# One place in memory for every moved operand: two kinds of activation slots in a single-core decoder step

## The chip, the core and the metric

The kernel runs on one core of one Trainium2 chip. The metric is device time in microseconds for one execution; three runs of the kernel before have a median of 1624.26 us (1624.0 to 1624.49). The profile is of one execution.

## The reference

One step of a one-layer decoder for 256 prompt tokens and 8 x 4 sample tokens, 288 tokens in all, with a model width of 2048. All arrays are float32. Cut to what matters:

```python
mod = (silu(c) @ w_ada + b_ada)          # 6 shifts, scales and gates of 2048, per group of tokens
h = rms(x, g_mix) * (1 + sc_m) + sh_m
proj = h @ w_in                          # 2048 x 9216: b, c, hc, u, v, ga, gb
z = c_gate * hc;  ya = b_gate * conv(z)  # short convolution, width 3
yb = gelu(u) * (causal_mix(rms(gelu(v))) + b_sg)
merged = sigmoid(ga) * (ya @ w_pa) + sigmoid(gb) * (yb @ w_pb)
x = x + gt_m * (merged @ w_out)
h2 = rms(x, g_ffn) * (1 + sc_f) + sh_f
gate, up = split(h2 @ w_ffn_in)          # 2048 x 11264
x = x + gt_f * ((silu(gate) * up) @ w_ffn_out)   # 5632 x 2048
```

The outputs are the normed x of both groups, the last rows of z, and the normed v.

## The kernel before

Everything is held with features on the 128 partitions and the 288 tokens along the free axis. A matrix product is cut into tiles of 128 x 128 weights; for each, the weights are loaded into TensorE (the stationary operand) and 288 columns of activations are streamed past them (the moved operand) into one of a few PSUM tiles (`pm`, `px`), which sums over the tiles of the inner dimension.

Float32 precision comes from three products for each tile, written in `triple` (L227 to L236). Both operands are split into a high part, rounded to the type fp32r, and the rest, a low part: the weights into `hi` and `lo` (`Blk.split`, ScalarE's cast at L453, VectorE's subtraction at L459 or L248), the activations into a pair that `split` makes (L299 to L304), or `modulate`, `make_h1` and `scaled_tile`. The three products are high by high (L229), high weights by low activations (L232), and low weights by high activations (L234). In the profile, `pm<-s,hi` at L229 and L232 names the moved operand `s` and the weights `hi`. There are 11,328 matmuls of this kind. Some of them are 298 columns wide: ten columns behind the tokens carry the shift of the modulation through the product.

The activations live in `slots`: 92 buffers that `slot` hands out, each 298 x 4 = 1,192 bytes per partition, whatever is stored in it. Some slots are moved operands (fp32r pairs). Others hold plain float32 results that TensorE does not read in this way: `sinkA` (L733 to L742) copies the first partial product of a column tile m of w_in out of PSUM into a slot, where it stays (`part[m]`) until a later step adds the rest (`sinkC`, `sinkB`, `sinkD`). For m < 48 the slot also keeps the ten extra columns, which `sinkC` and `rescale` use. Small tiles for a short time come from another pool, `tmp`, of five buffers.

In the built program the 92 slots stand 1,216 bytes apart, so that they start at four places modulo 256 bytes: the 11,328 moved operands stand at 32 (2,652 of them), 96 (2,524), 160 (3,196) and 224 (2,956). The weights `hi` and `lo` stand at 224 modulo 256, all of them.

The order of the matmuls on TensorE is the order in which the code writes them. The order on VectorE, ScalarE and SyncE is written by hand in the first part (until the step `free`), and set by a scheduler after it. Weights come from HBM over SyncE's queue into seven `raw` buffers; a buffer comes free when both casts have read it.

Of the kernel before, what the change touches and what calls it, by code (L numbers as in the profile page):

```python
# [8 lines left out]
F32 = mybir.dt.float32  # L9
F32R = mybir.dt.float32r  # L10
BF16 = mybir.dt.bfloat16
ALU = mybir.AluOpType
AF = mybir.ActivationFunctionType

P = 128
D = 2048
T = 288
TP = 256
TU = T + 10
NB = 8  # L20
NS = 4
NC = 9
DFF = 5632
SLOTS = 92
RAW = 7
LEAD = 12
LAG = 2
# [27 lines left out]
SINGLE = 10  # L55
FIRST = 16
ROOTLESS = 48
LATER = 48
ON_VECTOR = (2, 5, 7, 9, 10, 12, 14, 18, 19, 22, 23, 26, 27, 30, 32, 35, 37, 41, 43, 45, 47)
XCUT = (0, 1, 2, 6, 10, 14, 16)  # L60
# [24 lines left out]
def decoder_kernel(tc, d):  # L85
    nc = tc.nc
    from contextlib import ExitStack

    with ExitStack() as es:
        def pool(name, bufs=1, **kw):  # L90
            return es.enter_context(tc.tile_pool(name=name, bufs=bufs, **kw))

        pc = pool("const")
        pw = pool("wstream")
        pslot = pool("slots", SLOTS)
        ptmp = pool("tmp", 5)
        pps = pool("psum", 4, space=bass.MemoryType.PSUM)
        with tc.manual_schedule(engines={nc.tensor.engine}):
            _body(tc, nc, d, pc, pw, pslot, ptmp, pps)


def _body(tc, nc, d, pc, pw, pslot, ptmp, pps):
    ids = [0]

    def nm(s):
        ids[0] += 1
        return f"{s}_{ids[0]}"

    def const(name, shape, dt=F32):
        return pc.tile(shape, dt, tag=name, name=name)  # L110

    def slot(dt=F32, shape=(P, T)):
        return pslot.tile(list(shape), dt, tag="s", name=nm("s"), padded_shape=[P, TU])

    def tmp(n=T):
        return ptmp.tile([P, n], F32, tag="t", name=nm("t"), padded_shape=[P, TU])
# [7 lines left out]
    V, A, G, PE, SY = nc.vector, nc.scalar, nc.gpsimd, nc.tensor, nc.sync  # L124


    ct = const("ct", [P, 16, NC])
    A.dma_start(ct, d["c"])
    cp1 = const("cp1", [P, C1_END])
    A.dma_start(cp1, d["cpack1"])  # L130
# [19 lines left out]
    V.memset(mhalf, -0.5)  # L150
    cs = const("cs", [P, 16, 32])
    V.memset(cs, 0.0)
    ctt = const("ctt", [P, 16, NC])
    A.activation(ctt, ct, AF.Tanh, scale=0.5)
    V.scalar_tensor_tensor(ctt, ctt, 1.0, ct, ALU.add, ALU.mult)
    cs_made = V.tensor_scalar(cs[:, :, :NC], ctt, 0.5, None, ALU.mult)
# [128 lines left out]
    def behind(a, b):  # L285
        tc.add_manual_dep(
            a.ins,
            b.ins.name,
            mybir.DependencyInfo(mybir.DependencyClass.NoSync, mybir.DependencyReason.DATA),
            reason="program order",  # L290
        )

    def sam(ap):
        return ap.rearrange("p (b s) -> p b s", s=NS)

    def bc4(ap):
        return ap.unsqueeze(2).to_broadcast([P, NB, NS])

    def split(a, n=T):  # L299
        hi = slot(F32R, (P, n))  # L300
        A.copy(hi, a)  # L301
        lo = slot(F32R, (P, n))
        V.tensor_tensor(lo, a, hi.bitcast(F32), ALU.subtract)  # L303
        return hi, lo  # L304

    def normed(kt, rb):
        t = slot()
        V.tensor_tensor(t, x[:, kt, :], rb, ALU.mult)
        return t
# [419 lines left out]
        return Do(f)  # L729

    part, raws = {}, {}

    def sinkA(m, ps):  # L733
        t = slot(shape=(P, TU) if m < ROOTLESS else (P, T))
        part[m] = t[:, :T]
        w = T
        if m < ROOTLESS:
            raws[m], w = t, TU
        if m not in ON_VECTOR if m < ROOTLESS else m % 2 or m % 8 == 4:
            A.copy(t[:, :w], ps[:, :w])  # L740
        else:
            V.tensor_copy(t[:, :w], ps[:, :w])  # L742

    def sinkC(m, ps):
        if m not in raws:
            return sinkB(m, ps)
        t = raws.pop(m)
        V.scalar_tensor_tensor(t[:, :TP], ps[:, :TP], t[:, T : T + 1], t[:, :TP], ALU.add, ALU.add)  # L748
        rescale(m + 4, V.tensor_tensor(t[:, TP:T], ps[:, TP:T], t[:, TP:T], ALU.add))

    def rescale(m, after):
        if m in raws:
            t = raws[m]
            behind(V.tensor_tensor(t[:, :T], t[:, :T], S["rb1"], ALU.mult), after)  # L754
            V.tensor_tensor(sam(t[:, TP:T]), sam(t[:, TP:T]), bc4(t[:, T + 1 : T + NC]), ALU.add)

    def sinkX(m, ps):
        after = sinkB(m, ps)
        if m >= 68:
            rescale(m - 68, after)  # L760

    def sinkB(m, ps):
        return V.tensor_tensor(part[m], ps[:, :T], part[m], ALU.add)  # L763
# [318 lines left out]
    a0[1].defer = a1[1].defer = True  # L1082
    a0[1].half = lambda: warm(6)
    w0 = OneTile("w0", 0, xe.__getitem__, sinkA)
    wK = OneTile("wK", 0, xe.__getitem__, lambda j, ps: sinkA(SINGLE + j, ps))
    w0.hooks = {8: [a1[0].run], 11: [a1[1].run, second_tile]}
    many = (ROOTLESS - FIRST) // 8
    wA = [Blk("wA", i, (xe if i < many else h1).__getitem__, lambda m, ps: sinkA(FIRST + m, ps)) for i in range((72 - FIRST) // 8)]
    wB = [Blk("wB", i, rh1, lambda m, ps: sinkB(LATER + m, ps)) for i in range((72 - LATER) // 4)]
    wX = [Blk("wX", i, rh1, lambda m, ps: sinkX(LATER + m, ps)) for i in range((72 - LATER) // 4)]  # L1090
    wS = [Blk("wS", i, rh1, sinkC) for i in range(SINGLE // 2)]
    wC = [Blk("wC", i, rh1, lambda m, ps: sinkC(SINGLE + m, ps)) for i in range((LATER - SINGLE) // 2)]
    for b in wA[:many]:
        b.width = TU
# [56 lines left out]
    n = len(steps)  # L1151
# [167 lines left out]
```

## Time and profile before

| | |
|---|---|
| median of three runs | 1624.26 us |
| the profiled execution | 1624.22 us |
| its span, from first to last instruction | 1622.4 us |
| granted TensorE clock | 0.998 |
| TensorE busy | 1611.5 us (99%), 12,641 matmuls |
| VectorE busy | 1017.0 us (63%) |
| ScalarE busy | 737.3 us (45%) |
| HBM read | 352.74 MB, 219 GB/s over the span |

A busy time is the sum over which an engine had an instruction running. Matmuls overlap: one takes about 295 ns in the trace, but the next one starts long before it ends, so the time that a matmul costs is the distance from its start to the next start. "Chain" is the work that ended last, followed back from the end. A wait is told as who waited for whom.

### The profile page before, as it was taken

To read this page: it belongs to the slowest core of one execution; us is meant where nothing else is said; L and a number is where in the kernel's file an instruction comes from. 1 tells how busy PE (TensorE), PEld (TensorE's weight loads), DVE (VectorE), ACT (ScalarE), POOL (GpSimd) and SP (SyncE) were. 2 spreads that over 40 slices of the span, in tenths; PEclk is the share of its full clock that TensorE was granted. 3 is DMA by queue.
4 is the path that set the end of the run, shared out by engine and by line. 5 is a ranking of instruction groups with operands and counts; after the bars stand their busy time and mean duration, and the time that the engine had idled before them with its cause. 6 is when DMAs were issued, how large, how long until landed. Compare 5 with 4: busy or idle time off the path is not lost.

```text
span 1622.4 us, 31579 instructions
## 1 busy us (share of the span) xinstructions
PE 1611.5 (99%) x12641; PEld 1547.6 (95%) x12641; DVE 1017.0 (63%) x2194; ACT 737.3 (45%) x1360; POOL 21.2 (1%) x65
## 2 busy tenths in 40 slices
PE   9999999999999999999999999999999999999997
PEld 8998999899999999999999999999999999999997
DVE  6676788877755667667744555555555555555565
ACT  5533344643444434456643444444444444444454
POOL 0000000000000000011000000000000000000000
PEclk9999999999999999999999999999999999999999
DMA  9887866777778676654576556443564534645341
GB/s 376 324 319 287 312 237 212 273 279 295 288 281 337 260 271 227 236 176 157 193 304 251 217 177 208 159 172 110 169 224 156 173 117 161 226 157 172 109 162 59
DMA packets 59476, 357.88 MB, mean 221 GB/s; under 512 B 6720, under 2 KB 10176, under 8 KB 28608
## 3 DMA queue, kind: packets, MB, share of 16 engines
q1 hardware_dynamic: 59040, 355.73, 59.8%
q8 instruction: 99, 1.62, 0.4%
q14 instruction: 49, 0.40, 0.1%
q10 hardware_dynamic: 288, 0.13, 0.0%
HBM read 352.74 MB, written 3.09 MB: 219 GB/s over the span
## 4 chain that ended last, share of the span: by engine, by line
PE 98%; DMA 1%; DVE 0%; ACT 0%; DVEq 0%; issue 0%; ACTq 0%
PE pm L229 31%; PE pm L234 30%; PE pm L232 30%; PE ada L393 5%; DMA raw<-in_wK 1%; DMA raw<-in_w 0%; DVE st L1048 0%; DMA ct<-in_c 0%; PE px L232 0%; PE px L229 0%; PE px L234 0%; PE px L880 0%; PE px L879 0%; PE px L826 0%; PE px L203 0%; ACT hi L453 0%
## 5 line engine op out<-in xcount | busy, mean ns | idle before, releaser
L229 PE MATMUL pm<-s,hi 128*128 128x288 f32 (+1 forms) x3750 | 1109.1, 296 | 0.0
L232 PE MATMUL pm<-s,hi 128*128 128x288 f32 (+1 forms) x3750 | 1103.8, 294 | 0.0
L234 PE MATMUL pm<-s,lo 128*128 128x288 f32 (+1 forms) x3738 | 1102.2, 295 | 0.0
L453 ACT CAST hi<-raw 128x512 fp32r<-128x512 f32 (+1 forms) x963 | 587.2, 612 | 803.3 <-PE pm L232 762.6
L459 DVE TENSOR_TENSOR lo<-raw,hi 128x512 fp32r<-128x512 f32 (+1 forms) x849 | 578.7, 683 | 437.9 <-ACT hi L453 425.3
L229 PEld LDWEIGHTS pm<-s,hi 128*128 128x128 f32 x3750 | 705.7, 188 | 15.2 <-issue 13.0
L232 PEld LDWEIGHTS pm<-s,hi 128*128 128x128 f32 x3750 | 704.7, 188 | 0.0
L234 PEld LDWEIGHTS pm<-s,lo 128*128 128x128 f32 x3738 | 702.9, 188 | 0.0
L248 DVE TENSOR_TENSOR lo<-raw,hi 128x512 fp32r<-128x512 f32 x111 | 74.6, 675 | 29.6 <-ACT hi L453 28.9
L393 PE MATMUL ada<-raw,cs 128*32 128x512 f32 (+2 forms) x1152 | 88.3, 452 | 0.2 <-DMA raw<-in_a 0.2
L393 PEld LDWEIGHTS ada<-raw,cs 128*32 128x32 f32 x1152 | 30.9, 110 | 45.0 <-issue 41.1
L771 DVE TENSOR_TENSOR s<-pm,s 128x288 f32<-128x288 f32 x72 | 32.8, 456 | 19.9 <-PE pm L234 19.7
L301 ACT CAST s<-t 128x288 fp32r<-128x288 f32 (+1 forms) x76 | 32.9, 433 | 18.8 <-DVE t L803 12.4
L303 DVE TENSOR_TENSOR s<-t,s 128x288 fp32r<-128x288 f32 (+1 forms) x76 | 34.9, 459 | 6.5 <-ACT s L301 6.4
L343 DVE SCALAR_TENSOR_TENSOR x<-pm,mod,x 128x256 f32<-128x256 f32 x79 | 37.6, 475 | 0.0
L969 DVE SCALAR_TENSOR_TENSOR t<-t,pm 128x288 f32<-128x288 f32 x42 | 19.1, 454 | 20.9 <-PE pm L234 20.9
L763 DVE TENSOR_TENSOR s<-pm,s 128x288 f32<-128x288 f32 x48 | 21.8, 454 | 10.4 <-PE pm L234 9.5
L342 DVE TENSOR_TENSOR t<-pm,mod 128x32 f32<-128x32 f32 x79 | 15.2, 192 | 18.3 <-PE pm L234 18.2
L748 DVE SCALAR_TENSOR_TENSOR s<-pm,s 128x256 f32<-128x256 f32 x48 | 23.1, 480 | 4.1 <-PE pm L234 4.1
L754 DVE TENSOR_TENSOR s<-s,rb 128x288 f32<-128x288 f32 x48 | 21.5, 448 | 0.0
L171 ACT ACTIVATE t<-x 128x288 f32<-128x288 f32 x29 | 12.9, 445 | 17.4 <-DVE x L346 17.4
L176 DVE TENSOR_TENSOR acc<-acc,t 128x288 f32<-128x288 f32 x33 | 15.0, 455 | 8.2 <-ACT t L171 8.2
(164 smaller groups left out, 470.9 us busy)
## 6 DMA issues: line engine op xcount, KB each, us to landing
raw<-in_fi SPq DMA_DIRECT2D x84, 1024.0 KB, 4.8
raw<-in_a SPq DMA_DIRECT2D x64, 1024.0 KB, 7.9
raw<-in_f SPq DMA_DIRECT2D x64, 704.0 KB, 4.0
raw<-in_wD SPq DMA_DIRECT2D x34, 1024.0 KB, 5.4
raw<-in_aE SPq DMA_DIRECT2D x16, 1024.0 KB, 9.6
raw<-in_wo SPq DMA_DIRECT2D x16, 1024.0 KB, 6.0
raw<-in_wC SPq DMA_DIRECT2D x19, 768.0 KB, 4.3
raw<-in_pa SPq DMA_DIRECT2D x8, 1024.0 KB, 5.9
```

The source lines that it names most:

```text
L229: PE.matmul(out, wh, ah, start=first, stop=False)
L232: end_ = PE.matmul(out, wh, al, start=False, stop=turn and last)
L234: end_ = PE.matmul(out, wl, ah, start=False, stop=last)
L248: lows.pop(0)[1]()
L301: A.copy(hi, a)
L303: V.tensor_tensor(lo, a, hi.bitcast(F32), ALU.subtract)
L343: V.scalar_tensor_tensor(x[:, m, :TP], ps[:, :TP], mod[:, gt0 + m, 0:1], x[:, m, :TP], ALU.mult, ALU.add)
L393: PE.matmul(acc[32 * j : 32 * j + 32, :w], cs[:, kt, :], self.raw[:, o : o + w], start=kt == 0, stop=kt == 15, tile_position=(0, 32 * j), ...
L453: A.copy(hi, self.raw[:, s * 128 : e * 128])
L459: sub()
L748: V.scalar_tensor_tensor(t[:, :TP], ps[:, :TP], t[:, T : T + 1], t[:, :TP], ALU.add, ALU.add)
L771: V.tensor_tensor(a, ps[:, :T], a, ALU.add)
```

## The change

The slots are divided in two kinds. `slots` are now 56 buffers with a pitch of 320 elements (1,280 bytes, five times 256), and a slot that will hold an fp32r operand begins 7 elements (28 bytes) behind the buffer's start. `kept` is a new pool of 36 buffers of 288 elements (1,152 bytes) for the long-lived partial products of 36 column tiles, `LONG`: m = 24 to 27 and 40 to 71. Since a `kept` buffer has no room for the ten extra columns, the 12 of these tiles with m < 48 put them into a new constant, `extra`, with a copy of their own, and `raws[m]` holds the pair of both. The tiles `ct` and `ctt`, which were constants, come from the `tmp` pool.

In the built program all 11,328 moved operands then start at 92 modulo 256, and all their weights at 64 modulo 256.

```diff
-SLOTS = 92
+MAIN = 56
+KEPT = 36
+LEADIN = 7
+PITCH = 320
...
+LONG = tuple(range(24, 28)) + tuple(range(40, 72))
...
-        pslot = pool("slots", SLOTS)
+        pslot = pool("slots", MAIN)
+        pkept = pool("kept", KEPT)
...
     def slot(dt=F32, shape=(P, T)):
-        return pslot.tile(list(shape), dt, tag="s", name=nm("s"), padded_shape=[P, TU])
+        o = LEADIN if dt == F32R else 0
+        t = pslot.tile([P, o + shape[1]], dt, tag="s", name=nm("s"), padded_shape=[P, PITCH])
+        return t[:, o:] if o else t
+
+    def kept():
+        return pkept.tile([P, T], F32, tag="k", name=nm("s"))
...
-    ct = const("ct", [P, 16, NC])
+    ct = tmp(16 * NC).rearrange("p (k n) -> p k n", n=NC)
...
-    ctt = const("ctt", [P, 16, NC])
+    ctt = tmp(16 * NC).rearrange("p (k n) -> p k n", n=NC)
...
+    extra = const("extra", [P, sum(m < ROOTLESS for m in LONG), TU - T])
 
     def sinkA(m, ps):
-        t = slot(shape=(P, TU) if m < ROOTLESS else (P, T))
+        wide = m < ROOTLESS and m not in LONG
+        t = kept() if m in LONG else slot(shape=(P, TU) if wide else (P, T))
         part[m] = t[:, :T]
-        w = T
+        w = TU if wide else T
+        copy = A.copy if (m not in ON_VECTOR if m < ROOTLESS else m % 2 or m % 8 == 4) else V.tensor_copy
+        copy(t[:, :w], ps[:, :w])
         if m < ROOTLESS:
-            raws[m], w = t, TU
-        if m not in ON_VECTOR if m < ROOTLESS else m % 2 or m % 8 == 4:
-            A.copy(t[:, :w], ps[:, :w])
-        else:
-            V.tensor_copy(t[:, :w], ps[:, :w])
+            e = t[:, T:] if wide else extra[:, LONG.index(m)]
+            raws[m] = t, e
+            if not wide:
+                copy(e, ps[:, T:TU])
 
     def sinkC(m, ps):
         if m not in raws:
             return sinkB(m, ps)
-        t = raws.pop(m)
-        V.scalar_tensor_tensor(t[:, :TP], ps[:, :TP], t[:, T : T + 1], t[:, :TP], ALU.add, ALU.add)
+        t, e = raws.pop(m)
+        V.scalar_tensor_tensor(t[:, :TP], ps[:, :TP], e[:, :1], t[:, :TP], ALU.add, ALU.add)
...
     def rescale(m, after):
         if m in raws:
-            t = raws[m]
+            t, e = raws[m]
             behind(V.tensor_tensor(t[:, :T], t[:, :T], S["rb1"], ALU.mult), after)
-            V.tensor_tensor(sam(t[:, TP:T]), sam(t[:, TP:T]), bc4(t[:, T + 1 : T + NC]), ALU.add)
+            V.tensor_tensor(sam(t[:, TP:T]), sam(t[:, TP:T]), bc4(e[:, 1:NC]), ALU.add)
```

TensorE's, GpSimd's and SyncE's instructions stand in the same order as before, row for row. VectorE and ScalarE have six more instructions each, the copies into `extra`. On VectorE, where the column tiles m = 26 and 27 are copied out of PSUM (`pm` a PSUM tile, `s` a slot, `q` a sum of squares), there stood before:

```order
L248 TENSOR_TENSOR lo_614<-raw_134,hi_612 128x512
L742 COPY s_627<-pm_618 128x298
L742 COPY s_639<-pm_629 128x298
L592 TENSOR_TENSOR q_122<-q_122,q_123 128x1152
L248 TENSOR_TENSOR lo_638<-raw_134,hi_636 128x512
```

and now, with the changed file's line numbers:

```order
L258 TENSOR_TENSOR lo_619<-raw_138,hi_617 128x512
L750 COPY s_633<-pm_624 128x288
L755 COPY extra<-pm_624 128x10
L750 COPY s_646<-pm_636 128x288
L755 COPY extra<-pm_636 128x10
L602 TENSOR_TENSOR q_126<-q_126,q_127 128x1152
L258 TENSOR_TENSOR lo_645<-raw_138,hi_643 128x512
```

Each copy of 298 columns became one of 288 and one of 10, both ahead of the next instruction in VectorE's order. On ScalarE it is the same at m = 24 and 25. Before:

```order
L453 CAST hi_584<-raw_129 128x512
L740 COPY s_600<-pm_592 128x298
L453 CAST hi_609<-raw_129 128x512
L453 CAST hi_612<-raw_134 128x512
L740 COPY s_615<-pm_602 128x298
```

and now:

```order
L463 CAST hi_588<-raw_133 128x512
L750 COPY s_604<-pm_596 128x288
L755 COPY extra<-pm_596 128x10
L463 CAST hi_614<-raw_133 128x512
L463 CAST hi_617<-raw_138 128x512
L750 COPY s_620<-pm_607 128x288
L755 COPY extra<-pm_607 128x10
```

The casts of the next weights stand behind one short copy more.

More of the change, by code (lines that the diff above doesn't have):

```diff
@@ L98, in decoder_kernel, with _body @@
         with tc.manual_schedule(engines={nc.tensor.engine}):
-            _body(tc, nc, d, pc, pw, pslot, ptmp, pps)
-def _body(tc, nc, d, pc, pw, pslot, ptmp, pps):
+            _body(tc, nc, d, pc, pw, pslot, pkept, ptmp, pps)
+def _body(tc, nc, d, pc, pw, pslot, pkept, ptmp, pps):
     ids = [0]
```

## The prediction

> **What bounds the kernel now.** I read the page first, for the span, the engines and the chain that ended last, then the waits of TensorE.
>
> ```profile
> span 1622.4 us, 31579 instructions
> PE 1611.5 (99%) x12641; PEld 1547.6 (95%) x12641; DVE 1017.0 (63%) x2194; ACT 737.3 (45%) x1360; POOL 21.2 (1%) x65
> PE 98%; DMA 1%; DVE 0%; ACT 0%; DVEq 0%; issue 0%; ACTq 0%
> PE pm L576 <- POOL wb L570: 1.1, 1, 1.1
> PE px L203 <- DVE t L185: 0.6, 1, 0.6
> PE px L232 <- DVE s L692: 0.3, 1, 0.3
> PE ada L393 <- DMA raw<-in_a: 0.2, 1, 0.2
> PE pm L506 <- ACT s L682: 0.2, 1, 0.2
> ```
>
> 98% of the chain is TensorE, and all its waits together are 2.4 us. The time is therefore the number of matmuls times the distance of their starts. By form, the matmuls that the change touches are these (columns: line, engine, operation, output and operands, shape and count; busy us, mean ns):
>
> ```profile
> L229 PE MATMUL pm<-s,hi 128*128 128x288 f32 x3626 | 1071.5, 295 | 0.0
> L234 PE MATMUL pm<-s,lo 128*128 128x288 f32 x3626 | 1068.6, 295 | 0.0
> L232 PE MATMUL pm<-s,hi 128*128 128x288 f32 x3626 | 1066.5, 294 | 0.0
> L229 PE MATMUL pm<-s,hi 128*128 128x298 f32 x124 | 37.6, 303 | 0.0
> L232 PE MATMUL pm<-s,hi 128*128 128x298 f32 x124 | 37.2, 300 | 0.0
> L234 PE MATMUL pm<-s,lo 128*128 128x298 f32 x112 | 33.5, 299 | 0.0
> ```
>
> With the small groups they are 11,328. Now the groups in the window from 1200 to 1300 us, where nothing but them runs on TensorE:
>
> ```profile
> L234 PE MATMUL pm<-s,lo 128*128 128x288 f32 x253 | 74.6, 295 | 0.0
> L229 PE MATMUL pm<-s,hi 128*128 128x288 f32 x253 | 74.6, 295 | 0.0
> L232 PE MATMUL pm<-s,hi 128*128 128x288 f32 x252 | 74.1, 294 | 0.0
> ```
>
> 758 matmuls touch 100 us and the 0.3 us ahead of it, so one starts every 132.3 ns. For 11,328 that is 1,499 us, 92% of the span.
>
> Is there anything to gain in these 132 ns? The warming matmuls have the same 288 columns in bf16. In the window from 5.1 to 5.5 us, where they run one behind the other, and in short windows around single matmuls of the usual kind (218.75, 276.13, 225.49 and 227.88 us, in this order), the groups say:
>
> ```profile
> L576 PE MATMUL pm<-wb 128*128 128x288 bf16 x5 | 0.8, 286 | 0.0
> ...
> L229 PE MATMUL pm<-s,hi 128*128 128x288 f32 x1 | 0.3, 288 | 0.0
> ...
> L229 PE MATMUL pm<-s,hi 128*128 128x288 f32 x1 | 0.3, 288 | 0.0
> ...
> L229 PE MATMUL pm<-s,hi 128*128 128x288 f32 x1 | 0.3, 302 | 0.0
> ...
> L229 PE MATMUL pm<-s,hi 128*128 128x288 f32 x1 | 0.3, 302 | 0.0
> ```
>
> The same work, at a granted clock of 0.998, takes between 288 and 302 ns, and each value comes back where the same loop comes back. A matmul's duration and the distance to the next start rise together (295 with 132). So something that repeats with the operands costs 2 to 16 ns over the bf16 row, on average 294.7 - 286 = 8.7 ns. Setting the trace's matmuls beside the built program's operands in order (11,328 on both sides), I found no difference between those under which VectorE, ScalarE or the DMA queues were busy and the others (all within 0.5 ns of 132.2), which leaves the operands' addresses.
>
> **The change part by part.** *The common place.* It does not move one matmul; it can only change what each takes. Two parts of it must be held apart. The first is that all stand alike modulo 256. The trace has four places, 64 bytes apart; the mean distance to the next start is 132.3, 133.0, 132.2 and 131.5 ns at 32, 96, 160 and 224 (2,458 to 3,141 matmuls of the three groups of 3,626 in each). The best is 0.7 ns under the mean: 0.7 x 11,328 = 8 us. The second part is the 28 bytes. Before, moved operand and weights differed by 0, 64, 128 or 192; a distance of 28 is in no row of this trace. Its bounds are the rows above: if every matmul went like the bf16 row, 8.7 x 11,328 = 98 us are gained; like the two fast ones, (294.7 - 288) x 11,328 = 76 us; like the two slow ones, (302 - 294.7) x 11,328 = 83 us are lost. With all operands at one relation, each matmul is repeated alike, so the mean needn't stay in the middle. I take half of the way to the fast rows: 3.3 ns x 11,328 = **37 us gained**. That is a choice: the fast rows show that 288 can be had beside a weight load, but nothing shows that 28 bytes is the distance which gives it.
>
> What speaks against it is the last matmul ahead of a block of adaLN products, beside which no weights are loaded. The timeline at 881.3 us (start us, us):
>
> ```profile
> 881.23 0.19 PEld L234 LDWEIGHTS pm<-s,lo 128*128 128x128 f32 x1
> 881.36 0.29 PE L234 MATMUL pm<-s,lo 128*128 128x288 f32 x1
> 881.43 0.62 ACT L453 CAST hi<-raw 128x512 fp32r<-128x512 f32 x1 [5.29 <-DMA raw<-in_fi]
> 881.58 0.16 PEld L393 LDWEIGHTS ada<-raw,cs 128*32 128x32 f32 x8 [0.17 <-issue]
> ```
>
> The next load begins 0.22 us after that matmul's start. By short windows on it and on such a one at 292.4 us, they take:
>
> ```profile
> L234 PE MATMUL pm<-s,lo 128*128 128x288 f32 x1 | 0.3, 294 | 0.0
> ...
> L234 PE MATMUL pm<-s,lo 128*128 128x288 f32 x1 | 0.3, 299 | 0.0
> ```
>
> So a good part of the 8.7 ns is there without a load beside it, which is why I don't go further than half.
>
> [...]
>
> *Twelve copies of ten columns,* six on ScalarE and six on VectorE, all in the first 110 us. The nearest rows:
>
> ```profile
> L974 ACT COPY w<-pm 128x9 f32<-128x9 f32 x3 | 0.4, 160 | 0.0
> L693 DVE COPY mod<-end 128x9 f32<-128x9 f32 x2 | 0.3, 168 | 0.0
> 10.00:60.00 50.00, 49.44 (x520) 46.36 (x518) 37.95 (x87) 32.71 (x71) 1.23 (x1) 1.00 0.95 371
> 60.00:100.00 40.00, 40.00 (x400) 37.87 (x402) 23.48 (x52) 18.47 (x39) 0.00 (x0) 1.00 0.79 304
> ```
>
> 12 x 0.17 = 2 us of work. The work that hides it is TensorE's own: between 60 and 100 us VectorE is busy for 23.5 and ScalarE for 18.5 of 40 us, and TensorE for all of it. Without that cover, a PSUM tile given back 0.17 us later, or a cast queued behind a copy, would hold TensorE 12 times: 2 us. I take 0.
>
> *Slots, 56 and 36 in place of 92.* The count is the same and the order on the engines too, so a writer waits for a buffer's last reader as before, or for one that is done sooner or later by some matmuls. The closest new reuse is in the product with w_out, 18 matmuls (2.4 us) behind the last read by TensorE, in instructions which stand behind the sums of the same column tile; 0, at most 2 us. *ct and ctt* keep their instructions: 0. Slots that start 28 bytes later are also written by ScalarE and VectorE; at 45% and 63% busy neither is on the chain: 0.
>
> *What is late next.* ScalarE's casts of the weights wait for TensorE:
>
> ```profile
> ACT hi L453 <- PE pm L232: 762.6, 834, 5.6
> ```
>
> So a faster TensorE calls for weights sooner. In the row from 10 to 60 us the DMA engines are at 0.95 of their time and 371 GB/s; there the stream can't go faster, and what the 500 matmuls would gain, 500 x 3.3 ns = 1.7 us, I take off. From 60 us on their share is 0.79 and less, enough for 2%.
>
> The sum: 37 - 1.7 = 35 us; 1624.2 (the profiled execution: a span of 1622.4 and 1.8 around it, equal to the runs' median of 1624.26) - 35 = 1589, rounded to **1588 us**.
>
> **The rivals.** *No change.* The excess belongs to the fp32r stream itself, whatever is read beside it. For it: the rows without a load beside, 294 and 299, and that four places differ by 1.5 ns at most. Against it: 288 and 302 for equal work. The time: 1624 us, or 1616 to 1624 if only the 64-byte place counts.
>
> *Slower: a broken start.* All moved operands started at a multiple of 32 bytes before (32, 96, 160, 224); now all start 28 bytes behind one, with one column ahead of the next multiple. If the stream is fetched in pieces, every matmul fetches one more, and the start decides it for all. The price from the rows of 298 and 288 columns: ten columns cost 8, 6 and 4 ns, 0.6 ns each; half of a piece of eight columns is four, 2.4 ns, and 2.4 x 11,328 = 27 us: 1651 us. It decides as soon as the gain from the distance is under 2.4 ns. Against it: the start of a stream may be covered by the end of the one before.
>
> [...]
>
> *All the way:* the distance frees the streams of each other: 288 ns each, 1624 - 76 + 3 = 1551 us; it is the forecast's own far end.
>
> That the change doesn't do what it says is no rival: in the built program all 11,328 stand 28 bytes from their weights.
>
> **How the numbers follow.** The forecast, faster with its far end, 0.58; its own range is 1535 to 1615. No change 0.16. Slower 0.26: the broken start at 1651, or a relation that by chance is one of the bad ones, up to the slow rows. What a measurement of this kernel can tell from no change is about 0.2%, 3 us, which is 0.3 ns per matmul: little falls into it. So faster 0.57, same 0.16, slower 0.27. The range for eight in ten, 1535 to 1650, leaves out the way to the bf16 row (1526), and the worse half of the slower cases.
>
> **What would show it.** In the changed kernel the three large groups should have means near 291 ns, not 295, with a small spread: single matmuls alike, since all have one relation. A window without other work should have a start every 129 ns. TensorE's share of the chain should stay at 97% or more, with waits of a few us. Means of 295 would be the first rival; 297 and more, with wide matmuls in proportion, the second. If the means fall and the time doesn't, TensorE waits, and the row of its waits names the weights (DMA) or a slot. The prediction is wrong if the time is over 1621.

## The result and the profile after

The changed kernel takes 1600.44 us (median of four runs, 1600.36 to 1600.73) against 1624.26 us (four runs, 1624.00 to 1624.49); the ratio is 0.9854 (95% interval 0.9837 to 0.9871), 24 us faster. The page of the changed kernel (span, busy time of the engines, the chain that ended last by engine) and its waits of TensorE:

```profile
span 1598.6 us, 31602 instructions
PE 1587.1 (99%) x12641; PEld 1522.7 (95%) x12641; DVE 1016.1 (64%) x2200; ACT 735.6 (46%) x1366; POOL 20.8 (1%) x65
PE 96%; DVE 2%; DMA 1%; issue 0%; ACT 0%; DVEq 0%; ACTq 0%
...
PE pm L586 <- POOL wb L580: 1.1, 1, 1.1
PE px L213 <- DVE t L195: 0.8, 1, 0.8
PE px L242 <- DVE s L702: 0.3, 1, 0.3
PE pm L239 <- DVE s L989: 0.3, 1, 0.3
PE px L213 <- DVE q L602: 0.2, 1, 0.2
PE pm L516 <- ACT s L692: 0.2, 1, 0.2
```

TensorE has the same 12,641 matmuls, its waits come to 2.9 us (2.4 before), and its busy time fell by 24.4 us, the span by 23.8. So the matmuls themselves became cheaper. The groups by form (busy us, mean ns), and the groups in the window from 1200 to 1300 us:

```profile
L239 PE MATMUL pm<-s,hi 128*128 128x288 f32 x3626 | 1058.8, 292 | 0.3 <-DVE s L989 0.3
L242 PE MATMUL pm<-s,hi 128*128 128x288 f32 x3626 | 1055.8, 291 | 0.1
L244 PE MATMUL pm<-s,lo 128*128 128x288 f32 x3626 | 1055.7, 291 | 0.0
L239 PE MATMUL pm<-s,hi 128*128 128x298 f32 x124 | 37.1, 299 | 0.0
...
L244 PE MATMUL pm<-s,lo 128*128 128x288 f32 x258 | 75.1, 291 | 0.0
L239 PE MATMUL pm<-s,hi 128*128 128x288 f32 x257 | 74.8, 291 | 0.0
L242 PE MATMUL pm<-s,hi 128*128 128x288 f32 x257 | 74.8, 291 | 0.0
```

772 matmuls touch the window where 758 did. Counted from start to start over all 10,800 undisturbed ones of 288 columns, the mean distance fell from 132.19 to 130.01 ns, and the spread nearly vanished: from 125 to 144 ns before, 129 to 132 after (all but six). 2.18 ns x 11,328 = 24.7 us covers the whole gain. It comes evenly in the second half: over stretches of 400 matmuls the two traces part by 2.0 to 2.4 ns per matmul of this kind everywhere after 850 us, and by 1.4 to 2.8 ns in the stretches ahead of it.

### The profile page after: what moved, and what is told of

Same layout as the page of the kernel before. It is cut to its first block, busy times and chain, and to the rows that moved or that the text cites. A ratio compares the mean times of both kernels' runs of the same rounds, so it can differ in the third digit from the quotient of the medians.

```text
span 1598.6 us, 31602 instructions
## 1 busy us (share of the span) xinstructions
PE 1587.1 (99%) x12641; PEld 1522.7 (95%) x12641; DVE 1016.1 (64%) x2200; ACT 735.6 (46%) x1366; POOL 20.8 (1%) x65
## 4 chain that ended last, share of the span: by engine, by line
PE 96%; DVE 2%; DMA 1%; issue 0%; ACT 0%; DVEq 0%; ACTq 0%
PE pm L239 30%; PE pm L242 30%; PE pm L244 30%; PE ada L403 5%; DMA raw<-in_wK 1%; DVE lo L469 1%; DMA raw<-in_w 0%; DVE s L337 0%; DVE st L1061 0%; DVE s L318 0%; DMA t<-in_c 0%; DVE q L602 0%; ACT hi L463 0%; DVE t L331 0%; PE px L893 0%
## 5 line engine op out<-in xcount | busy, mean ns | idle before, releaser
L239 PE MATMUL pm<-s,hi 128*128 128x288 f32 (+1 forms) x3750 | 1095.9, 292 | 0.3 <-DVE s L989 0.3
L242 PE MATMUL pm<-s,hi 128*128 128x288 f32 (+1 forms) x3750 | 1092.3, 291 | 0.1
L244 PE MATMUL pm<-s,lo 128*128 128x288 f32 (+1 forms) x3738 | 1088.6, 291 | 0.0
L761 DVE SCALAR_TENSOR_TENSOR s<-pm,s 128x256 f32<-128x256 f32 x36 | 17.3, 481 | 2.8 <-PE pm L244 2.8
```

What stands on the lines that cost most here:

```text
L239: PE.matmul(out, wh, ah, start=first, stop=False)
L242: end_ = PE.matmul(out, wh, al, start=False, stop=turn and last)
L244: end_ = PE.matmul(out, wl, ah, start=False, stop=last)
```

## The experiments

Two kinds of kernel were run. Variants of the changed kernel, with one number different, say what the whole program does. Probes, which only stream matmuls of this kind with given starts of their operands and compute nothing of the reference, say what a single relation costs. In the probes "place" is the start of the moved operand in elements of 4 bytes, counted from the weights' place modulo 256 bytes. The probes' distances from start to start are means over the matmuls of one output tile without its first ones; where a tile does not repeat one triple, they move by up to 0.4 ns with the choice of these. A kernel's distances are means over its undisturbed matmuls of 288 columns. A "common place" is one at which all moved operands start.

Three theories were set against each other: that the distance from the moved operand to the weights decides (theory 1), that the moved operand's own start decides (theory 2), and that only the sameness of all starts decides (theory 3).

**A probe of places, and sameness alone.** The first probe in short:

```diff
+    scan("m", [(o, 0, o) for o in range(64)])            # the moved operand shifted by o
+    scan("w", [(0, o, o) for o in range(64)])            # the weights shifted by o
+    scan("n", [(o, 0, o) for o in range(0, 24)], cols=32)
+    scan("v", [(o, 0, o) for o in range(0, 24)], width=256)
+    scan("p", [(o, 0, o) for o in range(0, 16)], mixed=True)
```

> This kernel computes nothing of the reference: it only streams matmuls of the kernel's kind (fp32r, three for each pair of operands, a new load of 128 columns of weights for each) and writes zeros. The moved operand stands 0 to 63 elements (0 to 252 bytes) behind the weights modulo 256 bytes, 48 matmuls for each place (outputs m..); then the weights stand 0 to 63 elements behind the moved operand (w..); then the moved operand at 0 to 23 elements with loads of 32 columns of weights only (n..), and with 256 columns moved (v..); at last the moved operands jump between four places 64 bytes apart, all shifted by 0 to 15 elements (p..). Theory 1, the distance to the weights decides: means near 291 ns at 7 elements and 294 or 295 at 0, 16, 32 and 48; the w row at 57 elements (which is also a distance of 28 modulo 256) equals the m row at 7; with loads of 32 columns the differences shrink. Theory 2, the moved operand's own start decides: the w rows are all alike, and the n rows show the same differences as the m rows. Theory 3, the sameness decides: all m rows near 291, and only the p rows near 295.

Measured, ns from start to start (m, w, and n with loads of 32 columns):

```
place      0      1      2      3      4      5      6      7      8      11     15     23     37     39
m        131.5  133.4  134.4  131.1  131.7  133.3  135.5  130.0  133.4  130.0  133.3  130.0  140.1  130.0
n        131.1  133.3  133.3  130.0  133.4  135.1  130.0  130.0  130.1  133.3  129.3  130.0
w at   57: 129.9    w at 53: 136.5    all w: 129.9 to 136.7
p, mean by place modulo 4:   0: 132.7    1: 135.7    2: 134.2    3: 131.3
```

By their durations (count: minimum, median and maximum ns, first and last start), the places 6 (`mag`) and 7 (`mah`):

```profile
L138 PE MATMUL mag<-mh,wh x16: 295/295/297, 54.7 to 60.8; 128*128 128x288 f32 x16
L139 PE MATMUL mag<-ml,wh x16: 296/301/301, 54.8 to 60.9; 128*128 128x288 f32 x16
L138 PE MATMUL mah<-mh,wh x16: 290/291/293, 61.2 to 67.0; 128*128 128x288 f32 x16
L139 PE MATMUL mah<-ml,wh x16: 290/291/293, 61.3 to 67.2; 128*128 128x288 f32 x16
```

Four bytes decide over 5.5 ns. Place 7 is one of nine of the 64 that come to 130.0, and none is under it. No theory came through whole. Theory 2's "w rows all alike" fails (129.9 to 136.7). Theory 3 falls: equal places cost from 130.0 to 140.1. Theory 1 found its number, the weights shifted by 57 give 129.9, which is the same distance of 28 bytes; but the distance of 44 bytes gives 130.0 with the moved operand shifted (11) and 136.5 with the weights shifted (53). With loads of 32 columns the places still range from 129.3 to 135.1 (mean of places 1 to 23: 131.7 against 132.9), so a spread stays with a quarter of the load. But which places are dear changes with it: place 6 falls from 135.5 to 130.0, and place 11 rises from 130.0 to 133.3 (the correlation of the m and n rows over these 23 places is 0.2). So the load has a part in a place's price, or the output has, which is 32 rows instead of 128; this probe doesn't part the two. With 256 columns they range from 113.4 to 123.2, and there place 7 is no longer the best. In the p rows, where starts jump, the place modulo 4 elements (16 bytes) shows most clearly: 3 is the best, 1 the worst.

In the kernel, a lead-in of 0 leaves everything of the change but the shift:

```diff
-LEADIN = 7
+LEADIN = 0
```

> The changed kernel with a lead-in of 0 in place of 7 elements: all moved operands at one place modulo 256, which is that of the weights. Nothing else differs. Theory 1 (the distance of 28 bytes decides): the gain is lost, 1616 to 1630 us, with matmuls of 294 to 295 ns, all alike. Theory 2 (the start of the moved operand inside a piece): not 1600 either; faster than 1600 if a start at a round place is good, slower than 1610 if the odd start is. Theory 3 (sameness alone): 1600 us, with matmuls of 291 ns.

1619.17 us, ratio 0.9968 (0.9957 to 0.998), 131.66 ns from start to start, as in the probe (131.5 and 131.6 at place 0). The groups:

```profile
L239 PE MATMUL pm<-s,hi 128*128 128x288 f32 x3626 | 1068.7, 295 | 0.0
L242 PE MATMUL pm<-s,hi 128*128 128x288 f32 x3626 | 1065.8, 294 | 0.0
```

So 5 of the 24 us come with the common place and all the rest of the edit, the copies and pools included, and 19 with the 28 bytes. Theory 1 foretold 1616 to 1630; its "all alike" failed, since the starts lie 126 to 135 ns apart. Theory 2 had excluded what lies between 1600 and 1610, so it stood too. The next three runs were to part them.

**One element less, another place of the same kind, and several places.**

```diff
-LEADIN = 7
+LEADIN = 6
```

> The changed kernel with a lead-in of 6 elements (24 bytes) in place of 7, nothing else. Theory 1 (the distance to the weights, coarse): about 1600 to 1606 us, since 24 is near 28. Theory 2 (the start inside 16 bytes, as the probe has it: 135.5 ns at 6, 130.0 at 7): 5.5 ns more for each of 11,328 matmuls, 1655 to 1665 us, slower than before the change. Theory 3 (sameness): 1600.

1660.52 us, ratio 1.0222 (1.0206 to 1.0238): 36 us slower than the kernel before, 60 slower than the changed one, by a shift of four bytes. The groups show where:

```profile
L242 PE MATMUL pm<-s,hi 128*128 128x288 f32 x3626 | 1086.4, 300 | 0.0
L239 PE MATMUL pm<-s,hi 128*128 128x288 f32 x3626 | 1077.2, 297 | 0.0
L244 PE MATMUL pm<-s,lo 128*128 128x288 f32 x3626 | 1073.4, 296 | 0.0
```

From start to start it is 135.54 ns, the probe's 135.5. "Near 28" is worth nothing, and a common place can be worse than four mixed ones.

```diff
-LEADIN = 7
+LEADIN = 11
```

> A lead-in of 11 elements (44 bytes): a distance of 44 from the weights, but the same place modulo 16 bytes as 28. Theory 1 (28 is the distance that counts): slower than 1600, as at any other distance. Theory 2 with the probe's 130.0 ns at 11: 1600 us within 2. With the weights moved by as much in the first probe (53 elements behind, the same distance) it was 136.5 ns, so a distance alone would not give both.

1600.48 us, ratio 0.9852 (0.9837 to 0.9868), 130.01 ns: the changed kernel's time to 0.04 us at another distance.

```diff
-PITCH = 320
+PITCH = 312
```

> A pitch of 312 elements (1,248 bytes) in place of 320, lead-in 7: the moved operands stand at six places modulo 256 (28, 60, 124, 156, 188 and 252 bytes from the weights), all of them 12 modulo 16. Theory 3 (sameness modulo 256 is needed): back to 1616 to 1625 us. Theory 2, prices of single places from the first probe (130.0 at 7, 39, 47 and 63 elements, 133.3 at 15, 136.7 at 31): a mean of 131.6 ns, 1618 us; by the probe's row with jumping places at 3 modulo 4 (131.3 ns): 1615 us. If only the place modulo 16 counted: 1600.

1611.95 us, ratio 0.9923 (0.9905 to 0.9941), 131.05 ns, faster than both estimates. In the built program the operands stand at eight places and not six (92 and 220 bytes from the weights are the other two), 1,236 to 1,576 matmuls at each; with these the first probe's single prices have a mean of 131.4 ns, 1616 us. Without sameness modulo 256, but with all starts at 28 modulo 32 bytes from the weights, 12 of the 24 us are there. The other 12 come back with one place for all, but it is not shown that sameness brings them: the first probe has 130.0 ns at the one place and 133.3 and 136.7 at two of the eight, which alone would make such a difference.

**Both starts.** This probe shifts moved operand and weights independently by 0 to 19 elements; in the built program both begin 128 bytes behind a multiple of 256, which is a multiple of 32 too.

> This kernel computes nothing of the reference: matmuls of 288 columns and zeros as outputs. The moved operands start 0 to 19 elements and the weights 0 to 19 elements behind a multiple of 256 bytes, every pair of the two with 30 matmuls (outputs m..w..). If the distance between moved operand and weights decides (theory 1), all pairs at one distance are alike: 130.0 ns wherever the moved operand starts 7 elements behind the weights, and 135.5 wherever 6. If the moved operand's own start decides (theory 2), all pairs with it at 7 are alike, whatever the weights' start. If both count for themselves, neither holds: the mean over all weights' starts still falls from moved starts at 1 and 2 modulo 4 elements to those at 0 and 3, by 1 to 3 ns, and around that mean each pair has its own value.

The rows of the probe at the one distance of 28 bytes, with the moved operand at 7, 8, 9, 13, 14 and 15 elements (the first of the three products of each):

```profile
L153 PE MATMUL mhwa<-mh,wh x10: 290/291/293, 577.3 to 580.8; 128*128 128x288 f32 x10
L153 PE MATMUL miwb<-mh,wh x10: 293/293/293, 659.8 to 663.3; 128*128 128x288 f32 x10
L153 PE MATMUL mjwc<-mh,wh x10: 297/298/305, 743.5 to 747.2; 128*128 128x288 f32 x10
...
L153 PE MATMUL mnwg<-mh,wh x10: 299/300/302, 1078.8 to 1082.5; 128*128 128x288 f32 x10
L153 PE MATMUL mowh<-mh,wh x10: 295/295/295, 1163.8 to 1167.4; 128*128 128x288 f32 x10
L153 PE MATMUL mpwi<-mh,wh x10: 290/291/293, 1247.2 to 1250.7; 128*128 128x288 f32 x10
```

One distance gives everything from 290 to 305 ns, and the value comes back when both starts move on by 8 elements (7 and 15, 130.0 ns each; at a distance of -1 the pattern comes back after 4, but for its first two values). Of the 143 pairs that can be compared in this way (the one with the probe's first tile left out), some 135 come back within 0.3 ns; the others, all with the weights at 0, 1 or 2 elements, differ by up to 5.3 ns. In ns from start to start:

```
distance  7, moved at 7 8 9 ...:   130.0 130.0 136.2 133.3 133.3 130.0 136.7 133.3 | 130.0 130.0 136.2 133.3 133.3
distance -1, moved at 0 1 2 ...:   131.8 133.6 133.3 130.0 | 133.3 133.3 133.3 130.0 | 133.3 133.3 133.3 130.0 | ...
mean over all weights' starts, moved at   0: 133.3   1: 135.1   2: 133.3   3: 131.6   4: 132.3   5: 134.9   6: 133.7   7: 130.9
                                          8: 132.7   9: 134.6  10: 133.5  11: 131.9  12: 131.7  13: 135.1  14: 133.8  15: 130.5
```

Theories 1 and 2 both fall as they stood. The moved operand's own start carries 52% of the variance over the 400 pairs, the weights' start alone 1%, and the rest is in the pair of both. The best starts are 7 and 15 elements, 28 bytes into a stretch of 32: there 15 and 17 of 20 weights' starts give 131.1 ns or less. No pair is under 129.9.

**High and low parts at places of their own.** The third probe gives the two parts of the moved operand places apart from each other.

> This kernel computes nothing of the reference: matmuls of the kernel's kind with 288 columns and zeros as outputs. The high part of the moved operand stands 0 to 22 elements behind the weights' place, the low part 0 to 22 elements, every pair of the two with 30 matmuls (output names h..l..). If each start sets its own price (theory 2), a pair costs the mean of the two single places, and no pair is under 130.0 ns, the lowest of the first probe. If the step from one start to the next counts too, pairs of unequal places lie off that mean on both sides, and some are under 130 ns: single matmuls of 125 to 128 ns, all between unequal places, stand in the trace of the kernel before.

The steps between unequal starts count: of 529 pairs, three have 128.9 ns, which no common place has, and single pairs lie from 4 ns under to 5 ns over the mean of their two places. That mean explains a part: its correlation with the pairs is 0.5 (the probe's first tile left out). The high part, which is moved in two of the three products, weighs most: its start alone carries 48% of the variance, the low part's 10%, and the three best pairs have it at 11 or 19, places of 130.0 ns by themselves. A row of the pair 11 and 0 (high by high weights, high weights by low, low weights by high):

```profile
L153 PE MATMUL hlla<-mh,wh x10: 290/290/297, 1027.9 to 1031.4; 128*128 128x288 f32 x10
L154 PE MATMUL hlla<-ml,wh x10: 290/290/290, 1028.0 to 1031.5; 128*128 128x288 f32 x10
L155 PE MATMUL hlla<-mh,wl x10: 292/292/292, 1028.1 to 1031.6; 128*128 128x288 f32 x10
```

Two of the three pairs were run in the kernel (the first with this edit, the second with 19 and 12):

```diff
-LEADIN = 7
+LEADIN = (11, 0)
...
-    def slot(dt=F32, shape=(P, T)):
-        o = LEADIN if dt == F32R else 0
+    def slot(dt=F32, shape=(P, T), low=0):
+        o = LEADIN[low] if dt == F32R else 0
...
-        lo = slot(F32R, (P, n))
+        lo = slot(F32R, (P, n), 1)
```

> The changed kernel with the high parts 11 elements (44 bytes) and the low parts 0 elements behind the weights' place, in place of 7 for both; nothing else. The probe of pairs has 128.9 ns for it, 1.1 ns under the 130.0 at 7 and 7. If the probe holds in the kernel, where 16 and more pairs of operands take turns and PSUM is read out: 1600 - 1.1 x 11.3 = 1588 us. If sameness of all moved operands is what counts, 1605 us or more.

1589.89 us, ratio 0.9789 (0.9775 to 0.9802), 128.97 ns: faster than the changed kernel by 10.5 us, and the best version here. Its three products have means of their own, as in the probe:

```profile
L244 PE MATMUL pm<-s,lo 128*128 128x288 f32 x3626 | 1059.0, 292 | 0.0
L239 PE MATMUL pm<-s,hi 128*128 128x288 f32 x3626 | 1055.1, 291 | 0.1
L242 PE MATMUL pm<-s,hi 128*128 128x288 f32 x3626 | 1052.1, 290 | 0.0
```

> High parts at 19, low parts at 12 elements, the probe's other pair at 128.9 ns: 1588 us by the probe; 1605 or more if sameness counts.

1600.07 us, ratio 0.985 (0.9837 to 0.9864), 129.88 ns. Here the probe missed by 1 ns. The kernel's matmuls fall into several kinds, 126 to 136 ns, where the probe's repeat one triple; why this pair doesn't keep its rhythm in the kernel stays open.

**Width and type.** The last probe varies the width at four places, and streams bf16 at 288 columns from 24 starts (0 to 23 elements of 2 bytes) and at all widths from the first of them.

> This kernel computes nothing of the reference: matmuls only, zeros as outputs. Widths of 128 to 512 columns in steps of 16, with the moved operand 0, 6, 7 and 11 elements behind the weights' place (outputs f, place, w, width), then the same in bf16 with 288 columns at 24 places (b) and in bf16 at all widths (bw). If the excess over the bf16 rows is a price of each matmul's start, it is the same for 256 and 512 columns, some 7 to 17 ns; if it is paid along the stream, it grows with the width and is 1.8 times as large at 512 as at 288. In bf16 the places make no difference if only the rate of 4 bytes for each column brings the excess about.

The granted clock was 0.56 in the first 200 us of this probe, so the widths under 208 columns are left out. From start to start, ns:

```
columns     256     288     400     512
bf16       109.2   122.5   169.2   215.8
place 0    120.0   131.7   180.0   226.7
place 7    115.6   130.0   180.0   226.7
place 6    120.0   135.6   185.0   233.3
place 11   117.8   130.0   180.0   230.0
```

The excess of place 7 over bf16 is 6.4, 7.5, 10.8 and 10.9 ns; it grows less than the width, and that of place 6 too (13.1 at 288, 17.5 at 512). The best place depends on the width: at 400 columns place 0 is as good as place 7, and place 11 equals it at 288 and 400 columns but not at 256 and 512. At 208 and 224 columns all four places come to 111.6 or 111.7 ns. In bf16 the 24 places differ by 0.8 ns (122.5 to 123.3). A bf16 load of weights is shorter too, 98 ns in the trace against 187, so these rows don't show whether the stream's type or the load makes bf16 cheaper and indifferent to places.

## Why the prediction was right, and where it was not

**What bounds the kernel.** Right: the gain is only distance times count. TensorE has 96% of the chain, one point under what was foretold, since the chain now goes back through VectorE for 2%; its own waits stayed at 2.9 us.

**The excess belongs to the addresses.** Right for the part that varies, and now shown: one number in the code, LEADIN, sets the mean to 130.0, 131.7 or 135.5 ns, with nothing else changed. The larger part of the excess over the 122.5 ns of the width probe's bf16 rows stayed in every version tried: 132.2 ns before, and still 128.97 in the best.

**The size, 3.3 ns x 11,328 = 37 us.** This is the term that was mis-sized; it measured 24.7. Half of the way to the fast rows was hit to the nanosecond in duration: 291, as foretold. What failed is the sentence that duration and distance "rise together": the durations fell by 3.4 ns (294.5 to 291.1), the distances by 2.2 (132.19 to 130.01). The "start every 129 ns" is wrong by that 1 ns. In the kernels the difference between duration and distance moves between 161.1 and 162.3 ns; a sum should have been made from starts alone.

**The sign was luck.** The prediction said that nothing shows 28 bytes to be the distance that gives the fast rows. In the first probe 45 of the 64 common places are dearer than the 132.19 ns of the kernel before, and 24 bytes costs 36 us in the kernel. That the change gained time at all, and that half of the way was near, rested on no row of the trace; the chance of 0.58 for "faster" was high for a place not yet measured.

**The fast rows as a bound.** Right as a bound, wrong as a place one can stay at. In the trace before, all 370 matmuls of 288 ns stand between unequal starts. Short distances are not bound to these: with a lead-in of 0, one place for all, 708 of 10,820 matmuls start 126 or 127 ns apart, and the mean is still 131.66. No common place of the 400 pairs is under 129.9, and the pairs of unequal places reached 128.9 in the mean, with single steps of 126 and 127 paid for by 129 and 131 beside them. The rival "all the way", 1551 us, is not to be had with a common place of these.

**The matmul without a load beside it.** The prediction kept to half of the way because such matmuls had 294 and 299 ns. In the changed kernel the one ahead of the block at 870.0 us, by a short window, has

```profile
L244 PE MATMUL pm<-s,lo 128*128 128x288 f32 x1 | 0.3, 291 | 0.0
```

and so have all 18 of 288 columns ahead of such a block, 290 or 291. Their mean fell by 5.0 ns (295.6 to 290.6), that of the others of their line by 3.6 (294.7 to 291.1). So the caution pointed at the truth, that the moved stream itself is concerned, but drew the wrong conclusion: these matmuls had as much to gain as the others. With a lead-in of 6 they have 294.4 where the others have 296.0, so there the load beside may cost something.

**The rival "no change"** rested on the excess belonging to the stream. Of that excess 7.5 ns stay at 130.0, but the stream's price depends on where it starts, so the conclusion didn't follow. That the price is the same "whatever is read beside it" holds only in part: in the probe of both starts the weights' start alone explains 1%, but with loads of 32 columns in place of 128 (and an output of 32 rows) the mean over 23 places is 1.2 ns lower and place 6 is 5.5 ns lower, and with the moved operand at one place the weights' start moves the price from 129.9 to 136.7.

**The rival "a broken start"** has the wrong sign for this place. A start 28 bytes into 32 is the best in the mean over the weights' starts, not the worst. Its idea that the start decides for every matmul at once was right, and four bytes less give it its due: 1660.5 us, beyond its 1651. That the stream is fetched in pieces, of eight columns, was the author's assumption, and no run shows it. Nor is a start off a round place worse as such: over all weights' starts, moved operands 4 and 8 bytes behind a multiple of 16 cost more than those at one, 134.9 and 133.6 against 132.5 ns, but 12 bytes behind it they cost less, 131.4.

**Copies and slots at 0.** Right. The copies in the trace:

```profile
L755 DVE COPY extra<-pm 128x10 f32<-128x10 f32 x6 | 0.9, 158 | 0.0
L755 ACT COPY extra<-pm 128x10 f32<-128x10 f32 x6 | 1.1, 175 | 0.0
```

2.0 us of work, as worked out, and among TensorE's waits none goes back to them. The one new wait on a slot's writer, 0.3 us at L989, is for an instruction that reads a PSUM tile out.

**The first 60 us, 1.7 us taken off.** Too much. The row of the window from 10 to 60 us, which had 371 GB/s and 520 matmuls, only 295 of them of the changed kind and not 500:

```profile
10.00:60.00 50.00, 49.29 (x553) 46.20 (x543) 38.45 (x93) 32.91 (x76) 1.33 (x2) 1.00 0.97 380
```

The DMA engines moved a little more, 380 GB/s at a share of 0.97, against 371 at 0.95. Over the first 800 matmuls, about the first 70 us, the gain was 0.4 us where 364 of the changed kind would make 0.8, so about half was missing there, a term of 0.4 us. Whether the DMA took it is not shown: this execution was already 0.6 us behind at its 100th matmul, ahead of the first one of the kind; the one with a lead-in of 11 was not (0.1 us) and gained 0.5 us.

## What to carry to other kernels

In this kernel, where TensorE has 96% of the chain and most of its matmuls are fp32r, each with a new load of weights, the start of the moved operand was a free parameter worth several per cent: 1600 us at 28 bytes from the weights and 1660 at 24. No other kernel was run. The weights' start had a part in which start is good (129.9 to 136.7 ns with the moved operand at one place), and so had the width (place 11 equals place 7 at 288 columns and costs 2.2 ns more at 256). It could not be reasoned out here; a probe that streams the kernel's own triple over all starts, one short run, agreed with five of the kernels within 0.2 ns (lead-ins of 0, 6, 7 and 11, and the pair of 11 and 0; it came ahead of the runs at 6, 11 and the pair), and missed one pair by 1 ns; its single prices missed the eight mixed places by 0.3. Make such sums from start to start, not from durations, and try unequal places for operands that take turns: they gave the best version, 1589.9 us.

## What was not expected of the hardware

The steps are coarse: in the probe of both starts about three in four of the means are 130.0, 131.1, 132.2, 133.3, 134.4, 135.6 or 136.7 ns, multiples of a ninth of 10 ns; by an estimate from these means alone, that would be a step of 3.33 ns in one of the three products. The price repeats for some 135 of 143 pairs when both operands move on by 32 bytes. And bf16 streams of the same width, with 122.5 ns against 130.0 at best, differ by only 0.8 ns over 24 places, at least with bf16 loads beside them. What in the chip makes these steps was not tried.
